# Two-layer S5 and gated-attention block plus two hybrid layers on one core: GpSimd's elementwise work given to VectorE and ScalarE, and new matmul prices in the ordering model

## The chip, the cores and the metric

One core of a Trainium2 chip. Its engines run their own instruction streams, each in order: TensorE (PE, matrix products and transposes), VectorE (DVE), ScalarE (ACT), GpSimd (POOL) and SyncE (SP, which issues the DMAs). They wait for one another by semaphores. The metric is the device time of one execution in microseconds (us); lower is better. It is the median of three runs of the kernel before, and the profile is of one further execution.

## The reference

The input is one sequence of 256 tokens with 1024 features, all in float32. Four layers change it in turn. The change touches the first two.

```python
# layer 1
h = rms_norm(x, even_norm_g[i]); proj = h @ even_w_in[i]
q, k, v, z_a, u, z_b = split(proj)
q, k = rms_norm(q per head), rms_norm(k per head)
o_a = stick_breaking_attention(q, k, v) * silu(z_a)
o_b = s5_mixer(u, lambda, log_dt, b, c, d, w_glu, b_glu) * silu(z_b)
x = x + concat([o_a, o_b]) @ even_w_out[i]
# layer 2
h = rms_norm(x, odd_norm_g[i]); q, k, v, z, r = split(h @ odd_w_in[i])
log_a = log_sigmoid(r @ gla_w_gate[i] + gla_b_gate[i]) / 16
o = rms_norm(gla_chunked(q, k, v, log_a)) * silu(z)
x = x + o @ odd_w_out[i]
# layers 3 and 4 (hybrid): dilated attention and retention, gated, with shift, scale and gate from c; then a last norm
```

The S5 mixer is a linear recurrence over the tokens with a complex diagonal state for each of 32 groups of 16 channels. Its parameters enter as tables: powers of the discretised eigenvalue (`lambda_bar`), times the `b` and `c` matrices.

## The kernel before

The weights stream through: SP loads each tile of 128x2048 float32 numbers (`raw`, three slots), ACT copies it rounded to a shorter form (`whi`, in two halves of 1024 columns), and DVE subtracts the copy from the original to get the low part (`wlo`, four pieces of 512 columns). Each product with a weight tile is three matmuls: high by high, low by high, high by low. `proj_a` (PSUM tile `pa`) moves 512 weight columns past stationary tokens; `proj_b` (`pb`) moves 256 tokens past stationary weights.

Every layer is written as fibers, Python generators that yield instructions. `Prog.run` puts the instructions of all fibers in one order: next comes the one that could start first, by a model of the engines. The model's price of an instruction is made in `Engine.__getattr__` (lines 270 to 306), which is also where every instruction is recorded, so that the profile names line 275 for all of them. The order so made is then fixed for each engine. For DVE the model's price is

```python
i.cost = 0.066 + (0.52e-3 if one else 1.04e-3) * n + 0.063 * cols
```

with `n` columns, in us. Nothing in the model lets an operation of GpSimd slow one of DVE.

In the first layer the S5 mixer runs beside the projections q, k, v of two head halves (six pairs of weight tiles, 48 `pa` matmuls each; the first pair comes ahead of the others). `s5_prep` makes small tables of 32 columns on DVE (`s_w`, `s_W`, `s_L`) and, in `turns`, the cosines and sines (`s_room`). `s5_tables` makes, for each of four groups of states, the large tables: `ez` (`s5ez` less `s5t`), `f0` (`s5f`), the scan's factors `rho` (`s5rho`) and `F` (`s5F` less `s5t`); `s5_tab` makes each half of such a table. In the kernel before, all of these products run on GpSimd. `s5_piece` then works off a group: PE transposes `ez` (`s5ep`), multiplies by the input (`s5vp`) and by a rotation (`s5jp`); DVE turns the result by cosine and sine (`s5B`, `s5m`), runs the scan over the 64 chunks, turns it back (`s5V` on DVE, `s5m` on GpSimd), adds another PE product in a closing sum (`s5m<-s5jp,s5m`), and PE makes the group's output (`s5yp`) with `F`. Beside this run the head norms of q and k (`qk_evac`: a chain of operations of 8 columns, `rs`, then `qraw`, transposes `qtp` on PE, copies `qT`, `kT`) and the attention products (`sbz`, `stick_fiber`).

In the second layer `q_evac` and `k_evac` of `odd_layer` let GpSimd copy and scale small tiles (`qi`, `kc`, `km`).

## Time and profile before

| | us |
|---|---|
| median of three runs | 1059.82 |
| the runs | 1059.82, 1060.17, 1055.63 |
| span of the profiled execution | 1059.9 |
| PE busy in it | 1031.7 |
| DVE busy | 757.2 |
| ACT busy | 502.3 |
| GpSimd busy | 64.2 |

An engine counts as busy while it executes. PE's matmuls are pipelined: one begins before the last one has ended, so two numbers matter, the duration of a row and the spacing from one to the next. The views used below are the page of the execution; tables by stretches of time, with the granted clock of PE (1.00 is 2.4 GHz, 0.50 is 1.2 GHz, other values are means over both); timelines of one engine, where rows of one form that follow each other are merged (x4 means four of them, with the time from the first one's start to the last one's end) and where a bracket gives the idle time ahead of a row and what ended it; the chain of work that ended last; groups of instructions by form; and the list of waits.

### The profile page before, as it was taken

How to read it: one execution, taken by the hardware profiler on the slowest of the kernel's cores; microseconds unless marked ns; L12 is line 12 of the kernel's file. 1: busy time of each engine (PE TensorE's matmuls, PEld its weight loads, DVE VectorE, ACT ScalarE, POOL GpSimd, SP SyncE). 2: the span in 40 equal slices, each digit the busy share in tenths (PEclk: the TensorE clock that was granted, in tenths of full speed). 3: DMA queues.
4: the chain of work that ended last, by engine and by line, in shares of the span. 5: the costliest groups of instructions: out<-in, count | busy, mean ns of one | idle time of the engine just before them, and what ended most of it. 6: DMA issues, size and time to landing. Idle time of an engine off the chain costs nothing.

```text
span 1059.9 us, 17583 instructions
## 1 busy us (share of the span) xinstructions
PE 1031.7 (97%) x7058; PEld 948.3 (89%) x7058; DVE 757.2 (71%) x1607; ACT 502.3 (47%) x756; POOL 64.2 (6%) x79
## 2 busy tenths in 40 slices
PE   8989979999999999999999999999999999999997
PEld 7967769978899789999899999978999989999995
DVE  6996675968889776766588967674565658984565
ACT  6647427646634654434422443455453442343442
POOL 0146340000110000000000000000000000000000
PEclk9989899999999999999999999999999999999999
DMA  8641124463864658564444567445645444454541
GB/s 293 209 161 64 51 80 140 151 212 129 308 240 174 250 213 305 205 231 148 159 160 159 199 241 267 168 143 215 237 161 199 173 166 159 139 181 167 198 173 40
DMA packets 33501, 192.53 MB, mean 182 GB/s; under 512 B 8171, under 2 KB 9195, under 8 KB 11148
## 3 DMA queue, kind: packets, MB, share of 16 engines
q1 hardware_dynamic: 33132, 190.90, 50.6%
q8 instruction: 55, 0.90, 0.3%
q10 hardware_dynamic: 288, 0.52, 0.1%
q14 instruction: 26, 0.21, 0.1%
HBM read 189.31 MB, written 1.05 MB: 180 GB/s over the span
## 4 chain that ended last, share of the span: by engine, by line
PE 88%; DVE 8%; issue 1%; ACT 1%; DMA 1%; POOL 1%; SPq 0%; DVEq 0%; ACTq 0%
PE pb L275 52%; PE pa L275 21%; PE as L275 4%; DVE wlo L275 2%; PE ret L275 2%; DVE rs L275 2%; PE sbz L275 1%; DVE s_w L275 1%; PE s5yp L275 1%; PE ntp L275 1%; PE s5vp L275 1%; DMA cols<-in_cols_dram 1%; PE gsc L275 1%; PE qtp L275 1%; DVE s5B L275 1%
## 5 line engine op out<-in xcount | busy, mean ns | idle before, releaser
L275 DVE TENSOR_TENSOR wlo<-raw,whi 128x512 fp32r<-128x512 f32 x604 | 394.4, 693 | 166.0 <-ACT whi L275 161.2
L275 PE MATMUL pb<-H,whi 128*128 128x256 f32 x2688 | 494.6, 285 | 0.0
L275 ACT ACTIVATE whi<-raw 128x1024 fp32r<-128x1024 f32 x302 | 307.4, 1053 | 314.9 <-issue 161.6
L275 PEld LDWEIGHTS pb<-H,whi 128*128 128x128 f32 x2688 | 420.8, 192 | 3.0 <-issue 2.0
L275 PE MATMUL pb<-H,wlo 128*128 128x256 f32 x1344 | 382.6, 285 | 0.0
L275 PEld LDWEIGHTS pb<-H,wlo 128*128 128x128 f32 x1344 | 257.6, 192 | 0.5 <-issue 0.2
L275 PE MATMUL pa<-whi,H 128*128 128x512 f32 x576 | 187.4, 401 | 2.9 <-DVE H L275 2.9
L275 PEld LDWEIGHTS pa<-whi,H 128*128 128x128 f32 x576 | 109.2, 191 | 28.3 <-DVE H L275 5.2
L275 PE MATMUL pa<-wlo,H 128*128 128x512 f32 x288 | 114.7, 398 | 0.0
L275 PE MATMUL pb<-yy,whi 128*128 128x256 f32 x384 | 69.5, 283 | 0.0
L275 PEld LDWEIGHTS pa<-wlo,H 128*128 128x128 f32 x288 | 54.9, 191 | 11.3 <-issue 0.7
L275 DVE SCALAR_TENSOR_TENSOR acc<-raw,cact,acc 128x512 f32<-128x512 f32 x84 | 59.1, 745 | 4.4 <-DMA raw<-in_wall_dram 4.2
L275 PEld LDWEIGHTS pb<-yy,whi 128*128 128x128 f32 x384 | 59.9, 192 | 0.0
L275 PE MATMUL pb<-yy,wlo 128*128 128x256 f32 x192 | 54.3, 283 | 0.0
L275 PE MATMUL pa<-whi,mg 128*128 128x512 f32 (+1 forms) x144 | 41.1, 368 | 0.0
L275 PEld LDWEIGHTS pb<-yy,wlo 128*128 128x128 f32 x192 | 36.9, 192 | 0.0
L275 PEld LDWEIGHTS pa<-whi,mg 128*128 128x128 f32 x144 | 26.0, 188 | 5.1
L275 PE MATMUL pa<-whi,mix 128*128 128x512 f32 x96 | 30.2, 393 | 0.3 <-ACT mix L275 0.3
L275 DVE SCALAR_TENSOR_TENSOR rs<-rs 128x1 f32<-128x1 f32 (+3 forms) x144 | 28.5, 198 | 2.7
L275 DVE SCALAR_TENSOR_TENSOR tg<-tg,pb 128x512 f32<-128x512 f32 x16 | 11.0, 688 | 26.4 <-PE pb L275 26.4
L275 ACT ACTIVATE sqj<-x 128x512 f32<-128x512 f32 (+1 forms) x19 | 11.5, 608 | 35.7 <-DVE x L275 33.5
L275 PE MATMUL pa<-wlo,mg 128*128 128x512 f32 (+1 forms) x72 | 26.9, 374 | 0.0
(277 smaller groups left out, 1082.1 us busy)
## 6 DMA issues: line engine op xcount, KB each, us to landing
raw<-in_wall_dram SPq DMA_DIRECT2D x174, 1024.0 KB, 4.9
x<-in_x_dram SPq DMA_DIRECT2D x2, 512.0 KB, 5.9
raw<-in_wall_dram SPq DMA_DIRECT2D x2, 512.0 KB, 7.0
s5bc<-in_s5bc_dram SPq DMA_DIRECT2D x4, 256.0 KB, 2.5
gate<-in_bgate_dram SPq DMA_DIRECT2D x2, 512.0 KB, 5.6
c<-in_cst_dram SPq DMA_DIRECT2D x1, 896.0 KB, 7.1
cst<-in_cst_dram SPq DMA_DIRECT2D x1, 704.0 KB, 12.0
s_room<-s_room SPq DMA_DIRECT2D x16, 32.0 KB, 3.4
```

Source lines behind the costliest of these rows:

```text
L275: i.eng, i.emit = name, (lambda: real(*a, **k))
```

## The change

In the first layer the products of `turns`, all of `s5_tab`, the two differences of `s5_tables` and the product with the cosine in `s5_piece` move from GpSimd to DVE. `f0` and `rho` move to ACT: `rho` was a product with a mask that is zero at position 0 and one elsewhere, and becomes a memset of position 0 on GpSimd and a copy of the other 63. In the second layer the copies and scalings of `qi`, `kc` and `km` move to ACT. The prices of matmuls in the ordering model rise: 0.112 for a transpose, 0.2267 for 512 moving columns in the short form (0.2158 before) and 0.1201 for 256 (0.1092 before). Comments and docstrings are dropped, which moves later line numbers.

```diff
                 if op == "transpose":
-                    i.cost = 0.107
+                    i.cost = 0.112
...
-                    i.cost = (0.4167 * n + 2.5) * 1e-3 if rhs.dtype == F32R else max(0.214, (1.667 * n + 10) * 1e-3)
+                    i.cost = (0.4167 * n + 13.4) * 1e-3 if rhs.dtype == F32R else max(0.224, (1.667 * n + 4) * 1e-3)
...
-            yield pool.tensor_tensor(S.cosj[:, gs, :], f[:, gs].unsqueeze(2).to_broadcast([P, 8, 64]),
+            yield dve.tensor_tensor(S.cosj[:, gs, :], f[:, gs].unsqueeze(2).to_broadcast([P, 8, 64]),
...
-        yield g.pool.tensor_tensor(m(a), w4, b4, op=OP.mult)
+        yield g.dve.tensor_tensor(m(a), w4, b4, op=OP.mult)
...
-        yield pool.tensor_scalar(f0, bc[:, 2, :], g.sg, None, op0=OP.mult)
+        yield act.activation(f0, bc[:, 2, :], AF.Copy, scale=g.sg)
...
-        yield pool.tensor_tensor(ez, ez, m, op=OP.subtract)
+        yield dve.tensor_tensor(ez, ez, m, op=OP.subtract)
...
-        yield pool.tensor_tensor(rho, S.rho[:, gs].unsqueeze(2).to_broadcast([P, 8, 64]),
-                                 g.K("misc")[:, 64:128].unsqueeze(1).to_broadcast([P, 8, 64]), op=OP.mult)
+        yield pool.memset(rho[:, :, 0:1], 0.0)
+        yield act.activation(rho[:, :, 1:64], S.rho[:, gs].unsqueeze(2).to_broadcast([P, 8, 63]), AF.Copy)
...
-        yield pool.tensor_tensor(F, F, m, op=OP.subtract)
+        yield dve.tensor_tensor(F, F, m, op=OP.subtract)
...
-    yield pool.tensor_tensor(r3(m), cb, r3(B), op=OP.mult)
+    yield dve.tensor_tensor(r3(m), cb, r3(B), op=OP.mult)
...
-            yield pool.tensor_copy(qi[:, sl, 0:64], qd[:, sl, P:P + 64])
+            yield act.activation(qi[:, sl, 0:64], qd[:, sl, P:P + 64], AF.Copy)
...
-                yield pool.tensor_scalar(kc[:, i, 0:64], kc[:, i, 0:64], egl[:, 4 * i + 1:4 * i + 2], None, op0=OP.mult)
+                yield act.activation(kc[:, i, 0:64], kc[:, i, 0:64], AF.Copy, scale=egl[:, 4 * i + 1:4 * i + 2])
```

The order that comes out differs in some 330 rows of PE, 550 of DVE and 200 of ACT. Three places follow.

DVE, where the small tables `s_W` are ready and the large tables of the first group begin (`rs` is the head norm of k, first half; one piece of the difference):

```order
 L275 TENSOR_TENSOR s_w<-s_L,s_w 128x32 x4
 L275 TENSOR_TENSOR s_L<-s_w 128x32
-L275 SCALAR_TENSOR_TENSOR rs<-rs 128x8
+L275 TENSOR_TENSOR s5ez<-s_W,s5bc 128x16x16
 L275 TENSOR_TENSOR s_L<-s_w 128x32
 L275 TENSOR_TENSOR s_w<-s_L,s_w 128x32
-L275 SCALAR_TENSOR_TENSOR rs<-rs 128x8
+L275 TENSOR_TENSOR s5ez<-s_W,s5bc 128x16x16
 L275 TENSOR_TENSOR s_w<-s_L,s_w 128x32 x3
 L275 TENSOR_TENSOR s_L<-s_w 128x32
-L275 TENSOR_TENSOR rs<-rs 128x8
+L275 TENSOR_TENSOR s5t<-s_W,s5bc 128x16x16
```

The table products stand where the steps of the head norm stood, which move behind them.

PE, at the first transposes of `ez` and the transposes of that head norm (`qtp`), before:

```order
L275 MATMUL s5ep<-cst_76,s5ez 128x128 x4
L275 MATMUL pa<-whi,H 128x512
L275 MATMUL pa<-wlo,H 128x512
L275 MATMUL pa<-whi,H 128x512
L275 MATMUL qtp<-cst_76,qraw 128x128 x4
```

and after, where the first piece's output (`s5yp`) comes ahead of them:

```order
L275 MATMUL s5yp<-s_room,s5T 128x64
L275 MATMUL s5yp<-s5m,s5F 64x64 x2
L275 MATMUL qtp<-cst_76,qraw 128x128 x4
L275 MATMUL pa<-whi,H 128x512
L275 MATMUL s5ep<-cst_76,s5ez 128x128 x4
L275 MATMUL pa<-wlo,H 128x512
L275 MATMUL pa<-whi,H 128x512
L275 MATMUL qtp<-cst_76,qraw 128x128 x4
```

The transposes of the head norm moved from behind the first group's `s5ep` to behind that group's whole piece.

DVE, at the third closing sum and the head norm of k, second half, before:

```order
L275 TENSOR_TENSOR s5m<-s5jp,s5m 128x512
L275 TENSOR_SCALAR rs<-qss 128x8
L275 TENSOR_TENSOR wlo<-raw,whi 128x512
L275 TENSOR_SCALAR rs<-rs 128x8 x2
L275 SCALAR_TENSOR_TENSOR rs<-rs 128x8
```

and after:

```order
L275 SCALAR_TENSOR_TENSOR rs<-rs 128x8 x2
L275 TENSOR_TENSOR rs<-rs 128x8
L275 TENSOR_TENSOR s5m<-s5jp,s5m 128x512
L275 SCALAR_TENSOR_TENSOR rs<-rs 128x8
L275 TENSOR_TENSOR wlo<-raw,whi 128x512
L275 SCALAR_TENSOR_TENSOR rs<-rs 128x8
```

The norm began behind the closing sum; now most of its steps stand ahead of it.

## Rows read from the trace of the kernel before

**Rows 1.** The page: busy time of each engine, share of the span, instructions.
```profile
PE 1031.7 (97%) x7058; PEld 948.3 (89%) x7058; DVE 757.2 (71%) x1607; ACT 502.3 (47%) x756; POOL 64.2 (6%) x79
```

**Rows 2.** Table by stretches: length, busy time of each engine, clock, DMA share, GB/s.
```profile
core 0: us, PE busy (x) PEld busy (x) DVE busy (x) ACT busy (x) POOL busy (x), PEclk, DMA share, GB/s
...
53.00:79.50 26.50, 21.88 (x117) 18.06 (x116) 23.86 (x72) 13.18 (x25) 12.10 (x12) 0.87 0.48 161
79.50:106.00 26.50, 25.33 (x131) 19.27 (x130) 18.25 (x31) 20.48 (x44) 16.84 (x20) 0.94 0.18 64
106.00:132.50 26.50, 24.55 (x138) 19.72 (x136) 16.66 (x31) 12.44 (x26) 10.17 (x12) 0.87 0.15 51
132.50:162.90 30.40, 24.86 (x143) 19.28 (x144) 21.66 (x35) 8.21 (x20) 11.87 (x12) 0.94 0.22 71
162.90:1060.00 897.10, 885.42 (x6276) 829.34 (x6274) 634.11 (x1294) 415.20 (x575) 7.29 (x14) 1.00 0.53 189
```

**Rows 3.** Timeline of PE: start, time, row; the idle time ahead and its releaser.
```profile
62.46 0.66 PE L275 MATMUL s5ep<-cst,s5ez 128*128 128x128 f32 x4 [0.99 <-POOL s5ez L275]
...
67.45 1.09 PE L275 MATMUL qtp<-cst,qraw 128*128 128x128 f32 x4 [3.63 <-DVE qraw L275]
...
144.18 1.11 PE L275 MATMUL qtp<-cst,qraw 128*128 128x128 f32 x4 [3.27 <-DVE qraw L275]
```

**Rows 4.** List of PE's waits: for whom, us in total, times, longest.
```profile
PE qtp L275 <- DVE qraw L275: 8.8, 3, 3.6
...
PE s5yp L275 <- DVE s5m L275: 3.0, 2, 1.9
```

**Rows 5.** Chain of work that ended last: start, time, what; later in the program.
```profile
255.20 14.77 PE pa L275 x65
...
395.70 24.11 PE pb L275 x201
```

**Rows 6.** Timelines of DVE and GpSimd: operations beside GpSimd.
```profile
109.62 1.72 POOL L275 TENSOR_TENSOR s5m<-s_room,s5B 128x512 f32<-128x512 f32 x1
...
135.69 1.72 POOL L275 TENSOR_TENSOR s5ez<-s5ez,s5t 128x512 f32<-128x512 f32 x1
...
110.13 1.76 DVE L275 TENSOR_TENSOR s5V<-s_room,s5B 128x512 f32<-128x512 f32 x1
...
136.20 0.68 DVE L275 TENSOR_TENSOR s5m<-s5jp,s5m 128x512 f32<-128x512 f32 x1
...
137.95 1.21 DVE L275 TENSOR_SCALAR rs<-rs 128x8 int32<-128x8 int32 x2
```

**Rows 7.** GpSimd's groups by form: count, busy us, mean ns, idle before.
```profile
L275 POOL TENSOR_TENSOR s5ez<-s_W,s5bc 128x256 f32<-128x256 f32 x8 | 7.5, 952 | 16.5 <-DVE rs L275 16.5
```

**Rows 8.** Timelines of DVE and ACT: prices of forms like the added ones.
```profile
22.69 0.75 DVE L275 TENSOR_TENSOR H<-nf,H 128x256 fp32r<-128x256 f32 x2
...
25.73 2.50 DVE L275 TENSOR_TENSOR wlo<-raw,whi 128x512 fp32r<-128x512 f32 x4 [0.48 <-ACT whi L275]
...
149.84 0.68 DVE L275 TENSOR_TENSOR s5B<-s_room,s5V 128x504 f32<-128x504 f32 x1 [1.45 <-ACT s5V L275]
...
20.01 1.14 ACT L275 ACTIVATE H<-ntp,cols 128x128 fp32r<-128x128 f32 x4 [1.52 <-PE ntp L275]
```

**Rows 9.** Timeline of DVE: first head norm, last small table, first and last closing sum.
```profile
31.86 0.17 DVE L275 TENSOR_SCALAR rs<-qss 128x8 f32<-128x8 f32 x1
...
58.86 0.72 DVE L275 TENSOR_SCALAR s_W<-s_W,sgc 128x128 f32<-128x128 f32 x1
...
86.30 0.69 DVE L275 TENSOR_TENSOR s5m<-s5jp,s5m 128x512 f32<-128x512 f32 x1 [2.92 <-POOL s5m L275]
...
155.83 0.69 DVE L275 TENSOR_TENSOR s5m<-s5jp,s5m 128x512 f32<-128x512 f32 x1 [1.35 <-PE s5jp L275]
```

**Rows 10.** Timeline of PE at the start of the second hybrid layer.
```profile
708.28 0.50 PE L275 MATMUL pa<-whi,H 128*128 128x512 f32 x1 [1.22 <-DVE H L275]
```

**Rows 11.** Table by stretches: where the second layer used GpSimd.
```profile
265.00:291.50 26.50, 26.50 (x192) 23.66 (x192) 21.89 (x35) 16.81 (x18) 2.86 (x6) 1.00 0.81 307
```

More of the change, by code (lines that the diff above doesn't have):

```diff
@@ L981, in turns @@
             gs = slice(8 * b, 8 * b + 8)
-            yield pool.tensor_tensor(S.cosj[:, gs, :], f[:, gs].unsqueeze(2).to_broadcast([P, 8, 64]),
-                                     jv.unsqueeze(1).to_broadcast([P, 8, 64]), op=OP.mult)
+            yield dve.tensor_tensor(S.cosj[:, gs, :], f[:, gs].unsqueeze(2).to_broadcast([P, 8, 64]),
+                                    jv.unsqueeze(1).to_broadcast([P, 8, 64]), op=OP.mult)
         for b in range(4):
@@ L1058, in s5_tab @@
         b4 = bc[:, c, :].rearrange("p (q a c) -> p q a c", q=4, a=2)[:, :, a, :].unsqueeze(2).to_broadcast([P, 4, 4, 16])
-        yield g.pool.tensor_tensor(m(a), w4, b4, op=OP.mult)
+        yield g.dve.tensor_tensor(m(a), w4, b4, op=OP.mult)
 def s5_tables(g, S):
-    pool = g.pool
+    act, dve, pool = g.act, g.dve, g.pool
     for b in range(4):
@@ L1537, in evac @@
                 yield g.on("ed")
-            yield pool.tensor_copy(qi[:, sl, 0:64], qd[:, sl, P:P + 64])
+            yield act.activation(qi[:, sl, 0:64], qd[:, sl, P:P + 64], AF.Copy)
             for i in (2 * j, 2 * j + 1):
-                yield pool.tensor_scalar(qi[:, i, 64:128], qd[:, i, P + 64:T], egl[:, 4 * i + 2:4 * i + 3], None, op0=OP.mult)
+                yield act.activation(qi[:, i, 64:128], qd[:, i, P + 64:T], AF.Copy, scale=egl[:, 4 * i + 2:4 * i + 3])
             ready.add(("q", j))
@@ L1556, in evac @@
             for i in (2 * j, 2 * j + 1):
-                yield pool.tensor_scalar(kc[:, i, 0:64], kc[:, i, 0:64], egl[:, 4 * i + 1:4 * i + 2], None, op0=OP.mult)
-            yield pool.tensor_copy(km[:, sl, :, 64:128], ki.rearrange("p h (a t) -> p h a t", a=2)[:, sl, :, 64:128])
+                yield act.activation(kc[:, i, 0:64], kc[:, i, 0:64], AF.Copy, scale=egl[:, 4 * i + 1:4 * i + 2])
+            yield act.activation(km[:, sl, :, 64:128], ki.rearrange("p h (a t) -> p h a t", a=2)[:, sl, :, 64:128], AF.Copy)
             ready.add(("k", j))
```

## The prediction

> **What bounds the kernel now.** I read the page first: span 1059.9 us, TensorE (PE) busy 97% of it, GpSimd 6% [rows 1]. So PE sets the time, and a change elsewhere pays only where PE waits. The table by stretches says where: after 162.9 us PE is busy for 885.4 of 897.1 us, the 11.7 spread thin, at full granted clock, while between 53 and 162.9 us its busy time falls short and the granted clock is 0.87, 0.94, 0.87 and 0.94 [rows 2]. That is the first layer's S5 mixer, and the only place where GpSimd is busy for long. PE's own rows there show six idle times over 0.9 us: one of 0.99 that ends with GpSimd, and five that end with a VectorE (DVE) product, 8.8 in three for the head norms (the longest 3.63 and 3.27) and 3.0 in two for a closing sum [rows 3, 4], in all 12.8 us. The clock rows add a second loss: (0.13 + 0.06 + 0.13) x 26.5 + 0.06 x 30.4 = 10.3 us of full-clock time, the clock sitting on its lower level (1.2 GHz) for twice that. So of the 135.6 us from 27.3 to 162.9, where the 240 token-major products of the stretch end, about 112.5 are matmul work. A check from the other side: 240 pa products at 0.227 us (14.77/65), 96 pb at 0.120 (24.11/201) [rows 5] and the S5, transpose and attention products, 44 us at their closest spacings, make 110; switches between kinds of product take the other 2. **At most 23 us can be won there.**
>
> Why is DVE late? Its small operations stretch when GpSimd works. Two shifts of 128x8 numbers took 1.21 us at 137.95, beside GpSimd [rows 6]; an operation of that size took 0.17 at 31.86 with GpSimd idle [rows 9]. A 512-wide product of two SBUF tiles took 1.76 at 110.13 beside GpSimd's own 1.72 at 109.62. But the closing sum at 136.20, which reads PSUM and one tile, took 0.68 although GpSimd ran from 135.69 for 1.72 [rows 6]. The head norm at 138 is a chain of a dozen such operations: it held PE for 3.27 us.
>
> **The change, part by part.** *GpSimd's work goes.* In the S5 stretch 32 half tables of 256 columns, 16 products and differences of 512 and 4 scalings of 128 leave it; its tables took 0.95 us each in the first group of the list [rows 7]. The waits on it go, and so does the stretching of DVE.
>
> *DVE gains* 32 operations of 256 columns at 0.33 us (two in 0.75 us, less 0.08 of the last one's tail) = 10.7, and 16 of 512 at 0.60 (four in 2.50 us, less the tail) = 9.6 [rows 8]: **20.3 us**. No row shows a 256-wide DVE product with these broadcast operands. Bounds: 0.33 from below, and from above the 0.95 that GpSimd took for the same operands [rows 7]. I take 0.33, since the product of two strided operands of 504 columns took the usual 0.68 [rows 8].
>
> The Trainium skill, GPSIMD Engine Reference, section Engine selection, puts two-input elementwise work on GpSimd at about twice VectorE's time. An estimate by that page would be half of GpSimd's figure, 0.48 instead of 0.33, which would make the 32 tables 15.2 us; the sum here stays with the row.
>
> *ScalarE (ACT) gains* four scalings of 128 and four copies of 504 columns; four scaled copies of 128 took 1.14 [rows 8], and four times that is an upper bound for the others, so under 6 us. ACT is busy 8 to 20 of 26.5 to 30.4 us in the four stretches [rows 2]: nothing on the path. In the second layer 12 small copies move to ACT, some 3.5 us by the same row; PE is never idle there [rows 11], and the products that need them stand behind 87 more pb (10 us). I cost them at 0, and at 2 if that cover goes. GpSimd keeps small memsets. No transfer changes its engine.
>
> *DVE's new load against PE's.* Summing DVE's order from the first head norm (31.86) to the closing sum of each S5 piece at these spacings gives, before, 38.8, 57.1, 65.1 and 75.3 us; after, 44.1, 62.2, 85.2 and 95.5. Of the 75.3, 76 operations of 512 or 504 columns make 45.6, four scans 4.6, eight transposed copies 5.3, and the rest is small. The trace has the first of the four sums end at 87.0 and the last at 156.5 [rows 9], so DVE lost 16 us up to the one and 49 up to the other to stretching and waiting. What is left of that is read off the two orders, with one loss kept: up to the last small table (59.6 [rows 9], 27.7 us after the start) DVE lost 5.5 us against its sum of 22.2; I put 2.2 of them to GpSimd's four products there and keep 3.3.
> - First piece. DVE has 24.5 us by spacings up to there now (the four cosine products are its own), so tables start at 31.9 + 24.5 + 3.3 = 59.7, and 4.1 us of products later, at 63.8, PE can transpose them. PE arrives after 96 pb, 95 pa and 8 transposes, 34 us after 27.3, at 61.3 to 62: it waits 2 to 2.5. From there DVE leads the chain by under 1 us: closing sum at 79.8, where PE stands 49.3 us of work behind 27.3 plus 3.2 of waits.
> - Second. The key transposes, for which PE waited 3.63 us, now stand behind the first piece, so their norm is long done. DVE's two key copies hold the attention products for about 0.9; closing sum at 101.0, PE 0.4 behind its work.
> - Third. The rotary table and the head norm lie beside the piece: 0.4 at the query transposes, 1.1 at the closing sum, 126.1.
> - Fourth. The head norm that cost 3.27 now stands mostly ahead of the third closing sum. Another 0.4; closing sum at 139.9.
>
> So PE waits 6.4 instead of 12.8 us, the last S5 products start at 140.2, and 2.4 + 6 x 0.23 later the stretch ends at 144.0 instead of 162.9: **18.9 us won** at full clock. Two things come off. The clock fell in four of the stretches with idle times of 1 to 4 us; with half as much idle I take half the loss, **5.0**. And the chains of 8- and 32-wide operations wait for their own results (0.17 us [rows 9], where the sum takes 0.08 to 0.10 for all): for some 25 that now stand alone **2.0**.
>
> *The new matmul prices* (0.227 instead of 0.216 for 512 columns, 0.120 instead of 0.109 for 256) touch no instruction, only the order. They are the spacings of [rows 5]. Most places move by a few rows. One I can price: at the second hybrid layer's start PE idles 1.22 us for the norm [rows 10], since the transposes stand behind 94 pa products; they now stand behind 90, 0.9 us earlier. I count **1.0** for all of these; against that, any of some 300 moved rows may cost as much.
>
> Sum: 1059.9 - 18.9 + 5.0 + 2.0 - 1.0 = **1047.0 us**. The profiled execution is 0.1 us above the median of the three runs (1059.82), so no correction.
>
> **Rivals.**
> *Full recovery.* DVE stays ahead in the small chains and the clock stays up: 1059.9 - 18.9 - 1.0 = 1040. For it: the ordering model's DVE prices (0.598 for 512 columns) now equal the trace's and no engine stretches any more, so the order should be kept as planned. Against: DVE carries 95.5 us of work in the 108 us between 31.9 and 139.9, so it has little to catch up with.
> *Nothing measurable.* DVE is in order: a sum that waits for PE or ACT holds the low parts (wlo) queued behind it, and then the weights come late too. If each of the four pieces loses 3 us more that way, 12 us go: 1059. For it: before, PE and DVE already wait for one another by turns, as the closing sum that waits for PE 1.35 us shows [rows 9]; against: much of that was handed on from the stretched operations.
> *Slower.* The broadcast products cost DVE what they cost GpSimd, 0.95: 32 x 0.62 = 19.8 us more, the closing sum at 159.7, the stretch's end at 163.8 and, with 2 to 3 us of clock, 1062 to 1064. It decides from 0.33 + 18.9/32 = 0.92 us each. Against it is the strided 504-column row.
> The Trainium skill, Perfetto Trace Analysis, section Optimizing Scalar/DVE Operations, says that work may be moved off a saturated DVE to Scalar or even GPSIMD, with the warning that the two share a port and it might not help; by the first half the change goes the wrong way, which would be this rival, and [rows 6] side with the warning.
>
> **How the numbers follow.** Forecast 0.65 (1047, its own range 1042 to 1054), full recovery 0.17, nothing measurable 0.12, slower 0.06. The range 1039 to 1057 reaches into full recovery and most of the no-change case and leaves out the slower one. A measurement of this kernel tells about 0.5% from no change, 5.3 us: faster takes the forecast's but for its upper edge and the full recovery, 0.79; same 0.15; slower 0.06.
>
> **What would show it.** In the profile after: the closing sums near 80, 101, 126 and 140; the 128x8 operations at 0.17 throughout; table products at 0.33 to 0.42; PE's idle in the stretch 5 to 8 us, the largest ahead of the first S5 transpose; the granted clock mean between 53 and 144 above 0.95; from 145 on the same picture shifted by 13. Wrong if the table products take over 0.6, if PE idles over 12 us between 53 and 145, if DVE sits at 97% there and the wlo rows come late, or if the time changes after the first layer.

## The result and the profile after

The changed kernel took 1045.86 us (median of four runs, 1044.87 to 1047.58) against 1058.95 for the kernel before beside it (1055.63 to 1060.17): a ratio of 0.9886, 95% interval 0.9866 to 0.9906. The forecast was 1047.0, and faster. The profiled execution has a span of 1043.5 us and took 1045.43; some 2 us lie around the span in every run here.

The page, busy time of each engine, share of the span and instructions, to set beside [rows 1]:

```profile
PE 1025.4 (98%) x7055; PEld 942.5 (90%) x7055; DVE 758.2 (73%) x1655; ACT 508.8 (49%) x776; POOL 1.7 (0%) x15
```

GpSimd is all but gone. DVE carries 48 instructions more and is busy for 758.2 us, hardly longer than before: what it gained in work it lost in stretching. The table by stretches answers to [rows 2] (columns: length, busy time of each engine, clock, DMA share, GB/s):

```profile
53.00:79.50 26.50, 25.68 (x143) 20.26 (x142) 26.50 (x89) 14.39 (x29) 0.23 (x2) 1.00 0.48 167
79.50:106.00 26.50, 25.98 (x171) 21.76 (x170) 23.91 (x58) 21.38 (x45) 0.23 (x2) 1.00 0.30 100
106.00:132.50 26.50, 26.39 (x161) 20.57 (x160) 23.19 (x51) 15.88 (x33) 0.23 (x2) 1.00 0.24 81
132.50:146.00 13.50, 13.07 (x94) 10.99 (x94) 8.11 (x12) 8.23 (x11) 0.00 (x0) 1.00 0.29 88
146.00:1044.00 898.00, 883.64 (x6231) 825.92 (x6229) 630.90 (x1288) 413.59 (x581) 0.61 (x2) 1.00 0.53 188
```

Three things are to be seen. PE is nearly full between 53 and 146, where it lacked 4.6, 1.2, 2.0 and, up to 162.9, 5.5 us. The clock is 1.00 in all of them, where it was 0.87 to 0.94. And DVE is full (26.50 of 26.50) between 53 and 79.5 without PE waiting for it much. All that PE waited for between 27 and 146, for whom, us in total, times, longest:

```profile
PE s5jp L275 <- DVE s5V L275: 0.7, 2, 0.4
PE s5ep L275 <- DVE s5ez L275: 0.6, 1, 0.6
PE s5yp L275 <- DVE rs L275: 0.5, 1, 0.5
```

1.8 us, where the six rows of before made 12.8 [rows 3, 4]; the head norms (`qtp` for `qraw`) are not among them. The 240 token-major products of the stretch (48 of each of the five pairs behind the first) end at 140.5 us instead of 162.9, where the attention products begin:

```profile
140.30 0.39 PE L275 MATMUL pa<-whi,H 128*128 128x512 f32 x1
```

DVE's rows (start, time, row) show the first step of the first head norm, the new table products and the four closing sums:

```profile
29.07 0.17 DVE L275 TENSOR_SCALAR rs<-qss 128x8 f32<-128x8 f32 x1
...
56.31 0.42 DVE L275 TENSOR_TENSOR s5ez<-s_W,s5bc 128x256 f32<-128x256 f32 x1
...
75.02 0.72 DVE L275 TENSOR_TENSOR s5m<-s5jp,s5m 128x512 f32<-128x512 f32 x1
...
78.63 0.80 DVE L275 TENSOR_TENSOR s5F<-s_L,s5bc 128x256 f32<-128x256 f32 x2
...
96.25 0.69 DVE L275 TENSOR_TENSOR s5m<-s5jp,s5m 128x512 f32<-128x512 f32 x1
...
121.03 0.68 DVE L275 TENSOR_TENSOR s5m<-s5jp,s5m 128x512 f32<-128x512 f32 x1
...
135.64 0.69 DVE L275 TENSOR_TENSOR s5m<-s5jp,s5m 128x512 f32<-128x512 f32 x1 [0.68 <-PE s5jp L275]
```

The tables begin at 56.3, two of them take 0.80 us, and the sums end at 75.7, 96.9, 121.7 and 136.3, against 87.0 for the first and 156.5 for the last before [rows 9].

But the span fell by 16.4 us and not by the 22.4 by which the stretch ended earlier: **6 us were lost again behind it.** Cut at the first norm transposes (`ntp`) of each layer, the program before spent 231.7 us in the first layer and 818.5 in the other three; the changed one 210.0 and 824.6. Of the 231.7, about 1.4 us are that one execution's own: the clock was 0.76 there between 8 and 15 us, at the very start, and 1.00 in the profiles of all other runs, the one with GpSimd's work in its old place (prices_only) too. From the first transpose to the end of the first 48 products it took 17.6 us, and 16.1 in every other. What follows compares with 231.7 as it stands. Layer by layer, second to fourth, the same table for the kernel before:

```profile
241.40:356.10 114.70, 114.47 (x742) 102.65 (x742) 96.73 (x202) 60.05 (x94) 6.68 (x12) 1.00 0.61 220
356.10:705.50 349.40, 348.11 (x2508) 329.11 (x2508) 250.52 (x510) 156.07 (x207) 0.00 (x0) 1.00 0.56 203
```

and for the changed kernel:

```profile
218.90:335.80 116.90, 115.13 (x742) 102.89 (x742) 95.98 (x202) 63.73 (x106) 0.00 (x0) 1.00 0.60 217
335.80:687.00 351.20, 349.06 (x2505) 329.15 (x2505) 250.38 (x509) 154.98 (x207) 0.00 (x0) 1.00 0.57 202
```

The second layer is 2.2 us longer, the third 1.8, and the fourth (to the end of the span) 2.1, 356.5 instead of 354.4. What PE waits for there, over all three layers:

```profile
PE pa L275 <- DVE H L275: 2.1, 3, 1.1
PE ntp L275 <- DVE xn L275: 1.9, 6, 0.4
PE gate_p L275 <- issue: 0.8, 1, 0.8
PE gst L275 <- ACT kc L275: 0.8, 1, 0.8
PE ada_p L275 <- DVE acc L275: 0.2, 1, 0.2
```

Before, only the first of these lines was there in size (2.9 us, with 0.2 for `ntp`). Whether the moved work or the new prices did that is what the experiments had to tell.

### The profile page after: what moved, and what is told of

Read it like the earlier page. It is cut to its first block, busy times and chain, and to the rows that moved or that the text cites. A ratio compares the mean times of both kernels' runs of the same rounds, so it can differ in the third digit from the quotient of the medians.

```text
span 1043.5 us, 17569 instructions
## 1 busy us (share of the span) xinstructions
PE 1025.4 (98%) x7055; PEld 942.5 (90%) x7055; DVE 758.2 (73%) x1655; ACT 508.8 (49%) x776; POOL 1.7 (0%) x15
## 3 DMA queue, kind: packets, MB, share of 16 engines
HBM read 189.31 MB, written 1.05 MB: 182 GB/s over the span
## 4 chain that ended last, share of the span: by engine, by line
PE 85%; DVE 9%; ACT 2%; DMA 2%; issue 1%; SPq 0%; DVEq 0%; ACTq 0%
PE pb L275 50%; PE pa L275 21%; PE as L275 4%; DVE wlo L275 3%; PE ret L275 2%; PE sbz L275 2%; DMA raw<-in_wall_dram 1%; DVE rs L275 1%; PE s5yp L275 1%; ACT whi L275 1%; PE ntp L275 1%; DVE s5B L275 1%; DMA cols<-in_cols_dram 1%; PE s5jp L275 0%; ACT sb_sp L275 0%
## 5 line engine op out<-in xcount | busy, mean ns | idle before, releaser
L275 DVE TENSOR_TENSOR wlo<-raw,whi 128x512 fp32r<-128x512 f32 x604 | 389.2, 688 | 168.8 <-ACT whi L275 165.9
L275 PE MATMUL pa<-whi,H 128*128 128x512 f32 x576 | 183.0, 395 | 2.1 <-DVE H L275 2.1
L275 DVE SCALAR_TENSOR_TENSOR acc<-raw,cact,acc 128x512 f32<-128x512 f32 x84 | 58.8, 747 | 10.4 <-DMA raw<-in_wall_dram 10.3
L275 DVE SCALAR_TENSOR_TENSOR rs<-rs 128x1 f32<-128x1 f32 (+3 forms) x144 | 24.8, 172 | 2.8
```

The costliest lines, as they stand in the source:

```text
L275: i.eng, i.emit = name, (lambda: real(*a, **k))
```

## The experiments

Three theories stood at the start. **One:** the moves win in the first layer, since DVE's small operations stretch while GpSimd reads beside them, and the new prices lose behind it. **Two:** the moved work itself costs the 6 us (ACT's copies in the second layer). **Three:** it was never the stretching; PE and DVE just waited for GpSimd's results. The table holds all runs: the median, the ratio to the kernel before with its interval, and from the profiled execution the first layer (from its first `ntp` to the second layer's) and the rest.

| run | us | ratio | first layer | layers 2 to 4 |
|---|---|---|---|---|
| before | 1058.95 | 1 | 231.7 | 818.5 |
| changed | 1045.86 | 0.9886 (0.9866 to 0.9906) | 210.0 | 824.6 |
| moves_only | 1043.31 | 0.9861 (0.9843 to 0.9879) | 213.3 | 818.6 |
| prices_only | 1070.28 | 1.0117 (1.0095 to 1.0138) | 235.0 | 822.9 |
| prices_first | 1039.89 | 0.9835 (0.9811 to 0.9858) | 209.9 | 819.0 |
| late_256 | 1045.64 | 0.9880 (0.9864 to 0.9897) | 210.1 | 824.1 |
| bias_15 | 1046.00 | 0.9887 (0.9872 to 0.9902) | 211.6 | 825.1 |
| layer2_gpsimd | 1045.80 | 0.9885 (0.9861 to 0.9910) | 209.9 | 824.9 |
| lock_reads | 1076.65 | 1.0185 (1.0155 to 1.0215) | 239.2 | 823.9 |
| lock_writes | 1102.89 | 1.0428 (1.0407 to 1.0450) | 267.3 | 823.2 |
| lock_memsets | 1047.75 | 0.9902 (0.9879 to 0.9924) | 211.3 | 825.5 |
| tables_gpsimd | 1055.57 | 0.9980 (0.9965 to 0.9996) | 219.9 | 824.6 |
| tables_left_out | 1045.64 | 0.9882 (0.9865 to 0.9900) | 207.7 | 828.0 |
| tables_twice | 1063.00 | 1.0043 (1.0027 to 1.0059) | 225.5 | 823.8 |

### The two halves of the change apart

The moves without the prices (**moves_only**, diff against the changed kernel):

```diff
-                    i.cost = 0.112
+                    i.cost = 0.107
...
-                    i.cost = (0.4167 * n + 13.4) * 1e-3 if rhs.dtype == F32R else max(0.224, (1.667 * n + 4) * 1e-3)
+                    i.cost = (0.4167 * n + 2.5) * 1e-3 if rhs.dtype == F32R else max(0.214, (1.667 * n + 10) * 1e-3)
```

> The changed kernel with the old matmul prices in the ordering model (0.107 for a transpose, 0.2158 for 512 moving columns, 0.1092 for 256); all of GpSimd's work stays moved. After the change the 240th token-major product of the first layer ended near 140.5 us instead of 162.9, 22.4 us earlier, but the rest of the program took 903.0 us instead of 897.0. Theory one: those 6 us come from the new prices, which make the model issue the next layer's transposes ahead of the DVE step (xn) that they need, so PE idles at the layers' starts. Then this kernel takes 1040 to 1041 us, its stretch after the 240th product is back at about 897, and the waits of the norm transposes (ntp) for xn, 7 of them with 3.2 us after the change, are gone. Theory two: they come from the moved work itself (twelve small copies on ACT in the second layer, other states at the layers' starts). Then this kernel takes 1045 to 1047 and prices alone do nothing. Theory three, the prediction's own term: prices are worth 1 us of gain, this takes 1047 to 1048.

Measured 1043.31. The prices without the moves (**prices_only**) are the same lines the other way round, in the kernel before.

> The kernel before with the new matmul prices alone; all of GpSimd's work stays on GpSimd. Theory one (prices cost 6 us behind the first layer): 1063 to 1066 us, with PE's idle ahead of the norm transposes at the layers' starts, and the S5 stretch's end within 2 us of 162.9. Theory two (the moved work costs them): 1058 to 1060. Theory three, the prediction's own term: 1058.

Measured 1070.28, more than any theory had. The last column of the table settles where the 6 us come from: layers two to four take 818.5 and 818.6 us with the old prices, 824.6 and 822.9 with the new ones, wherever GpSimd's work is done. Theory one holds and two falls, for the second layer too: moves_only, with all the copies on ACT, spends 114.6 us there.

The first layer is a surprise of its own. The new prices lengthen it by 3.3 us while GpSimd works (235.0 against 231.7; 4.7 without the low clock at the start of the execution of before) and shorten it by 3.3 once it doesn't (210.0 against 213.3). With the moves and the old prices the last S5 output (`s5yp`) begins at 143.1 us instead of 136.6, and PE runs out of other work before the mixer's output (`mix`) is there. PE's waits from 140 us to the layer's end in moves_only:

```profile
PE pb L275 <- DVE mix L275: 1.9, 3, 0.9
PE pb L275 <- ACT mix L275: 0.8, 1, 0.8
PE s5jp L275 <- DVE s5V L275: 0.4, 1, 0.4
PE pa L275 <- ACT mix L275: 0.3, 1, 0.3
```

The changed kernel waits 0.4 us there in all. By the medians prices_only is 12 us slower than the kernel before, by the profiled spans 7.3 (1067.2 against 1059.9); some 3 of the difference are the profiled execution of before, which was a long one (below). Why the new order suits the first layer less while GpSimd works there stays open; its clock is lowest, 0.74, between 53 and 79.5 us.

Two separate effects can be had separately. **prices_first** uses the new prices in the first layer and the old ones behind it:

```diff
+    late = False
...
-                    i.cost = 0.112
+                    i.cost = 0.107 if Engine.late else 0.112
...
-                    i.cost = (0.4167 * n + 13.4) * 1e-3 if rhs.dtype == F32R else max(0.224, (1.667 * n + 4) * 1e-3)
+                    i.cost = (0.4167 * n + (2.5 if Engine.late else 13.4)) * 1e-3 if rhs.dtype == F32R else \
+                        max(0.214, (1.667 * n + 10) * 1e-3) if Engine.late else max(0.224, (1.667 * n + 4) * 1e-3)
...
             yield from even_layer(g, ev)
+            Engine.late = True
```

> The changed kernel with the new matmul prices in the first layer only; from the end of even_layer on the ordering model uses the old ones. So far: layers two to four, from the second layer's first norm transpose to the end, took 818.5 us in the kernel before and 818.6 with the moves and old prices, but 824.6 in the changed kernel and 822.9 with the new prices alone; the first layer, from its first norm transpose, took 210.0 in the changed kernel and 213.3 with the old prices. Theory one (these are two separate effects of the prices, a gain of 3 in the first layer's order and a loss of 6 behind it): 1040 us, the first layer at 210 and the rest at 818 to 819. Theory two (each order is a draw; a new mixture lands anywhere): the rest at 819 to 825 and 1040 to 1046 us.

Measured 1039.89, with 209.9 and 819.0 us: theory one to the us, and the fastest kernel of this study, 1.65% under the kernel before. Its second and third layers take 114.8 and 349.4 us, as in the kernel before (114.7 and 349.4).

### Which price, and through what

For each kind of matmul I took the median distance to the next start and summed what exceeds it between the layers' starts: 7.0 us in layers two to four of prices_first, 12.9 in the changed kernel. That difference, 5.9, covers the whole loss. By the product that came late it lies for the most part at `ret` (1.5 us), `ntp` (1.3), `gate_p` (1.1), `gst` (1.0), `as` (0.8) and `ada_p` (0.5), less 1.1 at the first products with `H`. All but `ntp` stand among the `pb` products of 256 columns. **late_256** gives back the old price of transposes and of 512 columns behind the first layer, and keeps the new one of 256 (and of fewer in the same form):

```diff
-(2.5 if Engine.late else 13.4)
+(2.5 if Engine.late and n > 256 else 13.4)
```

> New prices in the first layer; behind it old ones for transposes and 512 columns but the new one for 256 columns (0.1201). Layers two to four took 819.0 us with all old prices there (run prices_first) and 824.6 with all new. PE's excess over its closest spacings grew in the changed kernel beside pb products (gst 0.94, gate_p 0.98, ret 0.6 in each hybrid layer, ada_p 0.3 to 0.5, as 0.2 to 0.3 in each) by some 4 us and ahead of the norm transposes by some 1.5. Theory one (the price of 256 columns makes the first, the price of 512 the second): layers two to four at 822.5 to 823.5, 1043 to 1044.5 us. Theory two (the price of 512 alone matters, as it sets how far PE is believed to be at a layer's end): 819 to 820 there, 1040 us.

Layers two to four take 824.1 us. So theory two falls, and theory one had the share too small: the price of 256 columns or fewer, raised by 0.011 us, makes 5.1 of the 5.6 us between prices_first and the changed kernel. The `ntp` side was tried by itself with a smaller head start for the norms (**bias_15**):

```diff
-BIAS = -0.35
+BIAS = -0.15
```

> The changed kernel with BIAS, the head start that the ordering model gives the norms at a layer's end, at -0.15 instead of -0.35; new prices throughout. On PE it moves only the groups of norm transposes (ntp) at the layers' starts behind 3 to 9 more products. Theory one (these transposes placed too early are most of the 6 us that the new prices cost behind the first layer): layers two to four take 819 to 821 instead of 824.6 us, and the time is 1040 to 1043. Theory two (they are only the some 1.5 us that PE waits ahead of ntp there, and a later ntp costs as much again at the first product with H, since the model plans 1.5 and 2.0 us of idle there instead of 0.8 and 1.25): 1045 to 1047.

Measured 1046.00 and 825.1: no gain. The waits ahead of `ntp` fell from 1.9 to 0.2 us, and those ahead of the first product with `H` rose from 2.1 to 3.3, as theory two had it.

How a truer price loses can be read at two places. PE's rows at the third layer's `gate_p`, in the changed kernel (layer begun at 335.8), behind DVE's row of the sums `acc` that it reads:

```profile
395.19 2.74 DVE L275 SCALAR_TENSOR_TENSOR acc<-raw,cact,acc 128x512 f32<-128x512 f32 x4 [0.73 <-DMA raw<-in_wall_dram]
...
396.15 0.40 PE L275 MATMUL pb<-H,whi 128*128 128x256 f32 x2
397.37 1.10 PE L275 MATMUL gate_p<-acc,cst 128*128 128x512 f32 x2 [0.82 <-issue]
```

and in prices_first (layer begun at 334.0):

```profile
397.49 0.28 PE L275 MATMUL pb<-H,wlo 128*128 128x256 f32 x1
397.61 1.02 PE L275 MATMUL gate_p<-acc,cst 128*128 128x512 f32 x2
```

The old order has `gate_p` 63.6 us into the layer, the new one 61.6, idle time included: with the old price the model believes that PE gets through more `pb` in the time that the product's operand needs, puts more of them ahead, and on the chip, where each takes 0.12 us, PE arrives with time to spare. With the true price it arrives when the operand is due, and any delay shows. At `gate_p` the profile names no releaser, but the third of the four pieces of `acc`, the last one that the first product reads, ends at 397.27, and DVE had waited 0.73 us for its transfer. Ahead of `gst` in the changed kernel the delay is on ACT:

```profile
283.40 2.01 ACT L275 ACTIVATE whi<-raw 128x1024 fp32r<-128x1024 f32 x2 [2.85 <-DMA raw<-in_wall_dram]
285.31 0.58 ACT L275 ACTIVATE kc<-gkt 128x512 f32<-128x512 f32 x1
```

The copy of `kc` that `gst` needs stood behind two weight copies that waited for a transfer. In prices_first it came no earlier:

```profile
285.11 1.06 ACT L275 ACTIVATE whi<-raw 128x1024 fp32r<-128x1024 f32 x1 [5.08 <-DMA raw<-in_wall_dram]
286.07 0.58 ACT L275 ACTIVATE kc<-gkt 128x512 f32<-128x512 f32 x1
```

It ended 67.5 us into the layer there and 67.0 in the changed kernel. But PE came to `gst` 68.4 us into the layer and did not wait; in the changed kernel it was there at 66.3. So at these two places the low price worked as a margin against a late transfer; that it does so at the others is my reading. The runs show which price does it and where the time goes, not that no other order would do.

`kc<-gkt` is not one of the moved operations, and that the moved ones have no part in it was run too. **layer2_gpsimd** puts the twelve copies and scalings of `qi`, `kc` and `km` back on GpSimd:

```diff
...
-                yield act.activation(kc[:, i, 0:64], kc[:, i, 0:64], AF.Copy, scale=egl[:, 4 * i + 1:4 * i + 2])
+                yield pool.tensor_scalar(kc[:, i, 0:64], kc[:, i, 0:64], egl[:, 4 * i + 1:4 * i + 2], None, op0=OP.mult)
...
```

> The changed kernel with the small copies and scalings of the second layer (qi, kc, km) back on GpSimd; prices stay new. Theory one (the 0.84 us that PE waits for ACT's kc ahead of gst is all that these copies cost, the rest of the second layer's longer time is the prices'): that wait goes or becomes one on GpSimd, the second layer takes 116 instead of 116.9 us, and the time is within 1.5 us of the changed kernel's 1045.9. Rival (the copies on ACT push its weight copies back and cost the whole 2 us of the second layer or more): 1042 to 1044 us.

Measured 1045.80, the second layer at 116.8 us, `gst` still 0.47 late behind the same two weight copies. The copies cost nothing, on either engine.

### Stretching by itself

**lock_reads** gives the changed kernel back some 42 us of GpSimd work that nobody needs:

```diff
+def side(g, lk, n=4, first=None):
+    if first is not None:
+        g.pool.real.tensor_tensor(lk[:, 0:256], first, lk[:, 0:256], op=OP.mult)
+    for _ in range(n):
+        g.pool.real.tensor_tensor(lk, lk, lk, op=OP.mult)
...
         yield pool.memset(rho[:, :, 0:1], 0.0)
+        if b:
+            side(g, S.lk)
...
     yield pool.memset(r3(B)[:, :, 0:1], 0.0)
+    if b:
+        side(g, S.lk)
+    else:
+        side(g, S.lk, 8, S.W.rearrange("p a g t -> p (a g t)"))
```

> The changed kernel with 33 further products on GpSimd, one of 256 and 32 of 512 columns, from a private SBUF tile into itself, in the S5 stretch from the end of the small tables on; nobody reads them, no engine waits for them, and every other engine's instructions stand in the same order. At 1.72 us each they keep GpSimd busy for some 55 us, against 51 us before the change. Theory one (DVE's products of two SBUF tiles stretch while GpSimd reads SBUF): 128x8 operations go from 0.17 to 0.3 to 1.2 us, 128x512 ones to 0.9 to 1.8 beside GpSimd; DVE loses 10 to 17 us up to the fourth closing sum, PE idles 8 to 14 us instead of 1.8 in the stretch, the clock falls in some of its parts, the stretch ends at 150 to 158 instead of 140.5: 1053 to 1063 us. Theory two (what cost time before was only that others waited for GpSimd's results): 1045 to 1047 us, as without.

Measured 1076.65: 31 us slower than the changed kernel, where theory one had 7 to 17, and the other one (theory three of the list above) falls. DVE's rows beside GpSimd's products:

```profile
57.86 1.05 DVE L275 TENSOR_TENSOR s_L<-s_w 128x32 f32<-128x32 f32 x1
...
84.07 0.68 DVE L275 TENSOR_TENSOR s5m<-s5jp,s5m 128x512 f32<-128x512 f32 x1
...
86.97 1.52 DVE L275 TENSOR_TENSOR s_room<-s_room 128x512 f32<-128x512 f32 x1
88.41 2.97 DVE L275 TENSOR_TENSOR wlo<-raw,whi 128x512 fp32r<-128x512 f32 x2
```

A product of 32 columns takes 1.05 us instead of 0.2, one of 512 takes 1.5 instead of 0.69, and the closing sum, which has one operand in PSUM, 0.68 in the midst of it. DVE's busy time grows by 26.1 us (784.3 against 758.2). By stretches:

```profile
53.00:79.50 26.50, 20.37 (x98) 16.69 (x97) 26.35 (x75) 9.60 (x17) 10.65 (x9) 0.87 0.38 131
79.50:106.00 26.50, 23.09 (x133) 18.04 (x132) 24.08 (x33) 15.54 (x40) 13.48 (x12) 0.87 0.27 90
106.00:132.50 26.50, 22.72 (x110) 16.85 (x109) 25.87 (x50) 17.07 (x35) 8.24 (x9) 0.87 0.15 50
132.50:162.90 30.40, 24.11 (x140) 19.65 (x139) 24.52 (x43) 10.13 (x19) 9.91 (x10) 0.83 0.20 70
```

This is the picture of before [rows 2], with the clock at 0.87 and 0.83 where PE waits, but now with DVE nearly full throughout: it carries the 20 us of the moved work as well, so nothing of the stretching is absorbed.

The control was to keep GpSimd as busy with writing alone. The first one (**lock_writes**) put 32 memsets of 512 columns where four products had stood.

> The same, with each product of 512 columns replaced by eight memsets of 512 columns into the private tile, so that GpSimd is busy in the same places but reads nothing of SBUF (but for the first product, which waits for the small tables). Theory one (it is GpSimd's reading that stretches DVE): as the changed kernel, 1045 to 1047 us, 128x8 operations at 0.17. Rival (any work of GpSimd beside DVE does it, its writing too): slower than the changed kernel by 5 us or more, like the run with products.

Measured 1102.89, and the run says nothing on the question, by a fault of mine: I took eight memsets to be as long as one product, but 32 of them took 18.6 us where four products take 4.6 to 7.5, and the S5 chain's own memset stands behind them on GpSimd, which works in order:

```profile
DVE s5B L275 <- POOL s5B L275: 52.1, 3, 23.3
```

DVE's products were not stretched in it (`wlo` 689 ns); the 57 us by which it is slower are for the most part that wait. **lock_memsets** has nine memsets in each place, 18 in the first:

```diff
+    for _ in range(n):
+        g.pool.real.memset(lk, 0.0)
```

> The changed kernel with 72 memsets of 512 columns, 18 behind the first memset of s5B and nine behind each later memset of s5rho or s5B, into a private tile on GpSimd, in the places where the run with side products had 32 products; at the 0.58 us that a memset took in the longer run of memsets, 5.2 us behind each, so GpSimd is busy as long as with the products (42 us) and no longer holds the S5 chain's own memsets back for 52 us. Theory (a GpSimd that only writes doesn't stretch DVE's products of two SBUF tiles): 1045 to 1049 us, 128x512 products at 0.69, 128x8 at 0.16 to 0.17. Rival: a time near the 1076.7 of the run with products.

Measured 1047.75, with GpSimd busy 39.4 us between 53 and 132.5 and DVE's products beside it as if it were idle (the last row is from a group by form: count, busy us, mean ns):

```profile
57.12 10.58 POOL L1066 MEMSET side<- 128x512 f32 x18
...
57.57 0.20 DVE L275 TENSOR_TENSOR s_w<-s_L,s_w 128x32 f32<-128x32 f32 x1
...
78.28 1.28 DVE L275 TENSOR_TENSOR wlo<-raw,whi 128x512 fp32r<-128x512 f32 x2
...
L275 DVE TENSOR_SCALAR rot<-rot 128x256 f32<-128x256 f32 x3 | 1.5, 505 | 0.0
```

That last row is the exception. Some operations that read one SBUF tile only did stretch beside the memsets: the scalings of 128x256 (`rot`) took 505 ns on average instead of 295 in the changed kernel, a cast of that size 491 instead of 293, the 128x8 shifts of the head norm 340 instead of 165. That makes some 2 us of DVE, and the run is 1.9 us slower than the changed kernel (their intervals overlap).

So it is not GpSimd's being busy as such that cost the kernel before its time, but its products: beside them DVE's operations with two SBUF operands stretch, and beside writing alone they don't. The operations with one operand add a little to that beside either; the two shifts of [rows 6] are of this kind.

### DVE's load

**tables_gpsimd** puts the 32 half tables alone back on GpSimd:

```diff
-        yield g.dve.tensor_tensor(m(a), w4, b4, op=OP.mult)
+        yield g.pool.tensor_tensor(m(a), w4, b4, op=OP.mult)
```

The engines' orders are made anew with it and differ in a few dozen places, so the run is not the move of these products alone.

> The changed kernel with the 32 half tables alone (s5_tab) back on GpSimd, new prices; the differences, the product with the cosine, rho and f0 stay on DVE and ACT. DVE is relieved of 32 products of 0.42 us, GpSimd gains 32 of about 0.95, some 30 us of the stretch. Theory one (what GpSimd reads beside DVE is paid by DVE, and the more the fuller DVE is): PE waits for the tables and for DVE's stretched chains, 1055 to 1068 us, the granted clock below 0.95 in some of the stretches between 53 and 163. Rival (DVE's load is what limits the first layer, so the relief is worth more than the stretching): 1040 to 1046 us.

Measured 1055.57, the first layer 10 us longer than in the changed kernel: of the 21.7 us that the whole change wins there, the half tables, with the order that goes with them, carry nearly a half. GpSimd's own rows hold a lesson on its price:

```profile
56.13 1.21 POOL L275 TENSOR_TENSOR s5ez<-s_W,s5bc 128x256 f32<-128x256 f32 x2 [55.29 <-DVE rs L275]
...
63.04 2.87 POOL L275 TENSOR_TENSOR s5t<-s_L,s5bc 128x256 f32<-128x256 f32 x2
```

Two take 1.2 us at best and 2.9 at worst: GpSimd is held up by DVE as DVE is by GpSimd.

**tables_left_out** replaces each half table by a memset on GpSimd, with every other instruction in its place. DVE's busy time falls by 9.4 us (758.2 to 748.8), not by 32 x 0.42 = 13.5, since such products follow each other at 0.33 us:

```diff
-        yield g.dve.tensor_tensor(m(a), w4, b4, op=OP.mult)
+        i = g.dve.tensor_tensor(m(a), w4, b4, op=OP.mult)
+        i.emit = lambda d=m(a): g.pool.real.memset(d, 0.0)
+        yield i
```

> The changed kernel without the 32 half-table products on DVE: a memset on GpSimd writes zeros in the place of each (so the S5 tables E and F come out as zero; the output isn't the reference's), and every other instruction stands in the same order. DVE loses 32 x 0.42 = 13.5 us of work between 56 and 125 us. Theory one (after the change PE hardly waits for DVE in the S5 stretch, 1.8 us in all, so DVE's added load lies beside PE's work): at most 2 us faster, 1043.5 to 1046. Rival (DVE's load still sets the pace of the stretch, and PE's own work there only looks dense): 6 us or more faster, under 1040.

Measured 1045.64, as the changed kernel. In its profile (of an execution of 1047.45 us) the first layer is 2.3 us shorter; the later layers are 3.4 longer there, with `gst` 1.7 us late. **tables_twice** issues each of them twice:

```diff
+        i = g.dve.tensor_tensor(m(a), w4, b4, op=OP.mult)
+        once = i.emit
+        i.emit = lambda once=once: (once(), once())
+        yield i
```

> The changed kernel with each of the 32 half-table products issued twice on DVE, 0.84 instead of 0.42 us each, all else in the same order. This is about the price (0.92 us) from which the prediction's slower rival would have decided. The rival's arithmetic (each us of DVE in the stretch is a us of the stretch's end): 32 x 0.42 = 13.5 us slower, 1058 to 1060. Theory (DVE stood idle some 6 us of the 79.5 between 53 and 132.5, and its low parts of weights run ahead): half of it is taken up, 1050 to 1055, with PE's idle ahead of the s5ep transposes and of s5yp grown by that, and the granted clock below 1 in one or two of the stretches.

Measured 1063.00, 17.1 us slower than the changed kernel and slower than the kernel before; my expectation that half of it would be taken up falls, and the rival's was still a little low. Two rows of the table by stretches:

```profile
53.00:79.50 26.50, 22.15 (x105) 17.46 (x103) 26.09 (x89) 11.40 (x26) 0.11 (x1) 0.94 0.38 131
79.50:106.00 26.50, 24.75 (x141) 19.68 (x142) 22.49 (x46) 17.84 (x41) 0.23 (x2) 0.94 0.27 90
```

and PE's two longest waits in them (start, time, row, idle time ahead and its releaser):

```profile
62.40 0.66 PE L275 MATMUL s5ep<-cst,s5ez 128*128 128x128 f32 x4 [2.45 <-DVE s5ez L275]
...
79.75 1.27 PE L275 MATMUL s5jp<-s5V,cst 128*128 128x512 f32 x2 [2.12 <-DVE s5V L275]
```

PE waits 11.8 us in the first layer instead of 3.5, and the clock's 0.94 in four stretches costs 0.06 x (3 x 26.5 + 30.4) = 6.6 us more: 14.9 of the 15.5 us that the layer grew by. The two runs together say where the changed kernel stands: 9.4 us less busy time on DVE win 2.3 in the first layer, 13.5 us more (771.7 against 758.2) lose 15.5. It lies on the edge.

## Why the prediction was right, and where it wasn't

**The bound, the place and the direction held.** The gain lies in the first layer, nearly all of it in the S5 stretch. From the end of the first pair's products to that of the 240 behind them the kernel before took 135.7 us (27.2 to 162.9) and the changed one 115.6 (24.9 to 140.5): 20.1 of the 23 us that were put down as the most to be won. The other 2.3 of the 22.4 lie ahead of the stretch and are no merit of the change: 1.4 are the low clock at the start of that one execution, and 0.9 a start of the first transposes that lies anywhere from 8.7 to 9.9 us in the runs. By itself the move wins 18.4 us in the first layer (231.7 to 213.3, moves_only), 17 without that start; by the medians it wins 15.0 us in all (1058.27, the kernel before beside it, to 1043.31). The working's 18.9 was at full clock; 11.9 was left once clock and small chains had come off, so the move won more than was forecast. The reason given, that DVE's operations stretch while GpSimd works, and not those with a PSUM operand, is shown by lock_reads and lock_memsets, with GpSimd's products for its work: its memsets stretch no product.

**The price of the table products was right**: 0.33 us of spacing (two in 0.75 to 0.80), the lower bound. The 0.95 in [rows 7] was itself a stretched figure: undisturbed, two such products on GpSimd start 1.16 us before the next pair (tables_gpsimd), 0.58 each. The estimate by the Trainium skill (GPSIMD Engine Reference, section Engine selection), 0.48, was too high here, since it halved that stretched figure; the page's factor of about two between the engines agrees roughly with 0.58 to 0.33, which is 1.8.

**DVE's sums were right and their start was not.** From the first head norm to the first table DVE took 27.2 us (29.07 to 56.31), where 27.8 was worked out. But the norm began 2.8 us earlier than in the trace of before, since the first pair's products ended at 24.9 us instead of 27.2; the closing sums come 4.1, 4.1, 4.4 and 3.6 us ahead of the forecast, which leaves 0.8 to 1.6 beyond the earlier start. These forecasts do not hold the 2.0 for the small chains, which was added behind them: that term had nothing to pay for.

**PE's waits, 6.4 forecast, were 1.8**, with the largest where it was said to be, ahead of the first S5 transpose, but 0.6 and not 2 to 2.5. PE's work was put too low by about as much. From 27.3 to 144.0 there are 116.7 us, 110.3 without the waits: that is the check's 110, and the 2 us of switches between kinds of product, which the working itself counts in its 112.5, were left out. Measured, the same products took 115.6 less 1.8, which is 113.8. Start 2.4 us early, waits 4.6 less, work 3.5 more: that is the 3.5 us by which the stretch ended ahead of the forecast.

**The clock term failed.** Half of the 10.3 us of lost clock was to stay; none did. It was scaled with the idle time, and no single idle time longer than 0.6 us was left. tables_twice shows the other side: with idle times of 2.1 and 2.45 us the clock is 0.94 in the same stretches.

**The term for the new prices had the wrong sign.** It was put at -1.0, against which "any of some 300 moved rows may cost as much". Behind the first layer they cost 5.8 us (818.6 to 824.6 is 6.0, the opposite way round 819.0 to 824.6 is 5.6), in it they won 3.3. The step that failed is the one that priced a single place, the start of the second hybrid layer, and let it stand for all: there PE's idle ahead of the first product with `H` did fall, from 1.22 to 1.12 and not by 0.9, but the transposes then waited (0.24 us), and the places among the `pb` products were not looked at. The list of signs named "if the time changes after the first layer", and this is what happened.

**The number was good because errors met.** The span was to be 1047.0 and was 1043.5: up to the stretch's end 3.5 us of end time (2.4 of them the earlier start), 5.0 of clock and 2.0 of small chains too much were kept, 10.5 in all, and behind it 7 too little was charged. And the sum was made in the span without the 2 us that lie around it: the profiled execution of before took some 1061.8 us by that and not 1059.9, so it was 3 us longer than the median rather than equal to it. That the predicted time is within 1.2 us is owed to this too.

**The rivals.** Full recovery (1040) is what happened in the stretch, and more; the new prices took it back behind it. prices_first, without them there, has a span of 1038.2 against the 1040 of this rival, which was a span too; that its time is 1039.89 is the 2 us around the span. Nothing measurable did not come about: DVE's queue held no low parts back, PE having no `wlo` among its waits. The slower rival was the right mechanism with the right side: with every table issued twice, 0.80 us from the first start to the next row, the kernel is slower than before (tables_twice). Its point of decision is nearer than was worked out: 0.59 us more for each table (0.33 to 0.92) were to be bearable; by the two runs, 1045.86 with one issue and 1063.00 with two, which is 13.5 us of busy time more or 0.42 for each table, the 1058.95 of before is met at 0.42 x 13.1/17.1 = 0.32 us more, if the loss grows evenly in between, which no run shows. **What was costed at nothing** was nothing: ACT's copies (layer2_gpsimd), and nearly so DVE's load as such (2.3 us of the first layer in tables_left_out), though the cover of the latter was thinner than the text let one think.

## What to carry to other kernels

An engine that is busy 6% of the span can set the time of another one: look at what the same small operation costs beside it and alone, and cost a move by both, the work that is added and the stretching that goes. Before more work goes to an engine that is full in one stretch, try the same work twice and not at all; what less of it wins says little of what more of it costs. And prices in an ordering model are not only estimates: a price that is too low for the engine that sets the time can serve as a margin for all that feeds it, so test a truer price by itself and by stage.

## What the runs showed of the hardware

GpSimd's reading and DVE's products of two SBUF operands held one another up by about a whole instruction: beside side products of 512 columns a DVE product of 32 columns took 1.05 us instead of 0.20 (lock_reads), and two GpSimd products of 256 columns took 2.87 instead of 1.21 beside DVE (tables_gpsimd). The closing sum, with one operand in PSUM, took 0.68 beside them. GpSimd's memsets did nothing of the kind to products: `wlo` at 683 ns on average, 128x8 products at 158 (lock_memsets). The Trainium skill, SBUF — State Buffer, section Who interferes with whom, says that a DVE instruction with two SBUF inputs contends with GpSimd instructions that read SBUF and not with those that only write; the runs agree, with these numbers. What the memsets did stretch are operations with one SBUF operand: a 128x256 scaling took 505 ns instead of 295, a cast 491 instead of 293 (lock_memsets).

I had not expected how much it costs when DVE is full: 42.3 us of side reading in the stretch made the first layer 29.2 us longer, part of it through the clock, which fell to 0.83 to 0.87 where PE waited. And a memset of 512 columns on GpSimd took 0.58 us from one to the next in a row of 32, some three times what I had put down for it.
